# A hybrid encoder trunk on one core: the norm's affine part on VectorE, four raw weight buffers, and a newly searched order

## The chip, the core and the metric

The kernel runs on one core of one Trainium2 chip. The core has five engines that work side by side, each through its own queue in order: TensorE (PE) for matmuls, with its weight loads shown as PEld; VectorE (DVE); ScalarE (ACT); GpSimd (POOL); and SyncE (SP), which here only issues DMA transfers from the chip's memory (HBM) into the core's on-chip memory. Engines wait for each other through semaphores. The metric is the time of one execution in microseconds (us). Times of a kernel are given as the median of several runs; the profile is of one execution more, which has a time and a span (first to last instruction) of its own.

## The reference

Two layers act on x of 256 tokens by 1024 channels, in float32. Each layer:

```
z = x @ w_in[l]                                   # 1024 x 7440, split into the parts below
y_a = differential attention(aq, ak, av)          # 4 heads, all 256 keys
y_b = gated delta net(q, k, v, gate, a, b)        # convolution, then a triangular solve and a scan, both directions
y_c = windowed attention(cq, ck, cv)              # 8 heads, +-128 tokens
proj = einsum('btnc,ncd->btnd', stack(y_a, y_b, y_c), w_branch)
h = sum(sigmoid(gz) * proj) @ w_out
x = layer_norm(ALPHA * x + h, ln1_g, ln1_b)       # the first norm
gate, up = split(x @ w_up); gate = conv3(gate) + conv_b
f = (silu(gate) * up) @ w_down                    # the FFN, 2816 wide
x = layer_norm(ALPHA * x + f, ln2_g, ln2_b)       # the second norm
```

`layer_norm(v, g, b)` is `(v - mean) * rsqrt(var + 1e-5) * g + b` over the 1024 channels.

## The kernel before, in words

**Weights.** All large weights are packed on the host into blocks of 128 x 1024 float32 (512 KB). Each block is streamed once, in a fixed order, by SP. The function `weights` (and `take`, which calls it) brings a block in: a DMA into one of the `raw` buffers, of which there are RBUFS; ACT (or DVE, whichever the planner takes) rounds it to a shorter format as `hi`; DVE subtracts, `lo = raw - hi`, a pass of 128x1024. There are four buffers each of `hi` and `lo`. A raw buffer is free for the next load when `lo` is made. The activations are split alike: x in channel-major form is `xTh` and `xTl`. Each product is three matmuls, `hi*hi`, `hi*lo` and `lo*hi`, into the same PSUM bank (`mm3`). `proj_ch` makes channel-major products of a block pair; `token_major` makes token-major ones; `proj_tok` makes the two products that end in a norm (`wo` after the mixers, `fd` after the FFN), in 512-wide halves and for the two token tiles tt = 0, 1. The last blocks are kept, so that tt = 0 is done first, and the norm of tt = 0 runs beside the matmuls of tt = 1.

**The norm.** `Norm.part` adds the product to `ALPHA * x` and takes statistics on DVE. `Norm.tail` aggregates them, takes the power -0.5 of the variance on GpSimd (`pow_nhalf`, tile `s_tail`), makes the normalized `xh` (`q_tail` in the profile) on DVE, transposes it on PE (`ch_tail`, `at_tail`), applies gain and bias per channel (`e_tail`), and splits the result into `xTh` and `xTl`; the next matmuls need these. `Norm.finish` makes the same normalized values in token-major form: x = xh * gain + bias, in place, for the residual sum of the next norm, one whole half-layer later. Gain and bias stand spread over all partitions in four `ya` buffers of 128 x 512, loaded by `ln_params` with DMAs that GpSimd issues. `finish` runs for three of the four norms (the last writes its output itself): two tiles, two halves, two passes, eight instructions of 128x512 a norm, 24 in all.

**The order.** Nothing is issued when the code is read. Every call is recorded in `Plan` as an operation with an engine (or two to choose from, `either`), a price from `_cost`, and what it depends on. `Plan.emit` gives each operation a rank: the length of the longest chain of prices and latencies from it to the end, plus `urgent` (HASTE 60 or HASTE0 39 in the tails, BOOST 8 for weights), plus an entry of the table PRIO that belongs to its label, such as `(1, 'solve')` or `(0, 'gz', 8)`. `Plan.schedule` then simulates the five engines: it always takes the operation that can start first by the simulation, and among those that can start at the same moment on an engine the one of highest rank. The order that comes out is the order of each engine's queue on the chip; within a queue nothing overtakes. Weight blocks keep their stream order (`ORDER`), and PRIO moves a block's other work. A DMA is simulated as an issue, a transfer (`_cost`), a latency (`op.lat`) and, where a buffer has to come free first, DMA_ISSUE more. The simulation slows PE to half for a slot of 3.41 us (TICK) after a slot with little matmul work.

Every operation is issued from one helper, so all lines of the profile say L191; the tiles tell the instructions apart (`lo_take` is the `lo` of a block, `s_tail` the small tiles of a tail, and so on). GpSimd also makes the decay matrices of the delta net (`x_decay`, `D_decay`, `N_decay`) and small powers.

Of the kernel before, what the change touches and what calls it, by code (L numbers as in the profile page):

```python
# [10 lines left out]
F32 = mybir.dt.float32  # L11
F32R = mybir.dt.float32r
# [3 lines left out]
ALU = mybir.AluOpType  # L16
# [3 lines left out]
P = 128  # L20
# [25 lines left out]
SPOT = {('ft', 0, 0): 'g', ('ft', 0, 1): 'g', ('ft', 0, 2): 'yc', ('ft', 1, 0): 'g', ('ft', 1, 1): 'g', ('ft', 1, 2): 'yc', ('av', 1, 0): 'h16'}  # L46
DIRECT = False
WHOLE = ()
PRIO = {(1, 'a', 0): 2.3, (0, 'ckv', 0): -3.3, (0, 'gz', 8): 4.3, (1, 'wb', 7): -1.6, (0, 'k', 'ab', 0): 1.4, (1, 'cq', 0): 2.7, (0, 'gz', 9): -1.8, (1, 'k', 'q', 1): 8.1, (0, 'gz', 7): -2.0, (1, 'solve'): -4.6, (1, 'c', 'cq', 0): 2.5, (1, 'k', 'k', 1): -2.8, (0, 'aq', 1): -5.9, (0, 'gz', 3): 3.5, (0, 'ab', 0): -7.3, (0, 'gz', 10): 1.9, (0, 'c', 'ckv', 0): 1.8, (0, 'c', 0): -2.1, (0, 'k', 'gate', 1): 0.2, (0, 'q', 0): -7.1, (0, 'a', 2): 3.4, (1, 'v', 0): -4.1, (1, 'gz', 7): -1.0, (1, 'a', 'aq', 0): 4.5, (0, 'k', 0): -6.2, (0, 'q', 1): -7.6, (0, 'solve'): -2.7, (1, 'aq', 1): -4.7, (1, 'a', 'aq', 1): -1.4, (0, 'wb', 1): -0.6, (1, 'q', 1): 5.3, (0, 'gate', 0): 7.8, (0, 'a', 0): -0.7, (0, 'wb', 7): -1.0, (1, 'k', 'v', 0): -6.5, (1, 'wb', 2): 3.6, (0, 'a', 3): 2.0, (1, 'c', 0): 3.5, (1, 'k', 'v', 1): -5.3, (0, 'k', 'v', 1): -8.6, (1, 'c', 3): 3.4, (1, 'gate', 1): 5.4, (1, 'scan'): -1.6, (1, 'a', 2): 6.9, (1, 'av', 0): 5.6, (1, 'wb', 9): 2.5, (1, 'gz', 6): 1.6, (0, 'gz', 0): 1.3}
LOADS = (11, 12, 12)  # L50
PIECES = 2
PAIRS = ("s", "yc")
# [7 lines left out]
           "ACT": {"PE": 0.27, "ACT": 0.14, "DVE": 0.14, "POOL": 0.18, "SP": 1.42},  # L60
           "DVE": {"PE": 0.26, "ACT": 0.2, "DVE": 0.13, "POOL": 0.18, "SP": 1.22},
           "POOL": {"PE": 0.2, "ACT": 0.15, "DVE": 0.1, "POOL": 0.11, "SP": 0.2}}
DMA_ISSUE = 1.2
TICK = 10.24 / 3
FULL = 3060
ENGINES = ("PE", "ACT", "DVE", "POOL", "SP")
# [5 lines left out]
def _columns(ap):  # L72
    return math.prod(c for _, c in ap.ap[1:])


def _cost(eng, name, outs, ins, args, kw):

    n = max(_columns(ap) for ap in (outs[:1] + ins))
    if name == "dma_start":
        return 1.04 if eng == "POOL" else max(0.1, math.prod(c for _, c in outs[0].ap) * 4 / 3.6e5)  # L80
    if eng == "PE":
        if outs[0].offset // outs[0].ap[0][0]:
            return 0.0223
        wide = outs[0].dtype == F32 and ins[0].dtype == F32
        n = _columns(outs[0])
        slow = 4 if wide and name != "transpose" or ins[0].dtype == F32R and n < 256 else 2 if wide else 1
        return max(n * slow / 2400, 0.025) + 0.0023
    psum = [ap.space == PSUM for ap in outs[:1] + ins]
    if eng == "ACT":
        t = (0.05 if any(psum) else 0.093) + _columns(outs[0]) / 1200  # L90
        return t + 0.093 * sum(isinstance(kw.get(k), bass.AP) for k in ("scale", "bias", "accum_out"))
    if name == "memset":
        return 0.035 + n / 1200 if eng == "POOL" else 0.01 + n * SIZES[outs[0].dtype] / 3840
    if eng == "POOL":
        if kw.get("op") == ALU.pow:
            return 0.3 + 0.165 * n
        return (0.06 + n / 960) if name == "affine_select" else 0.1 + n / 570
    full = [ap for ap in ins if _columns(ap) > 1]
    fast = 1
    if len(full) == 1 and not any(psum) and name in ("tensor_copy", "tensor_scalar"):  # L100
        fast = 4 if full[0].dtype == F16 else 2
    return 0.069 + n / 960 / fast + 0.061 * sum(_columns(ap) == 1 for ap in ins)
# [26 lines left out]


class _Op:
    __slots__ = ("eng", "call", "cost", "deps", "known", "outs", "lat", "tiles", "new", "rank", "table", "start", "end", "urgent", "ways", "succ", "left", "ready", "group", "banks", "load", "columns", "label")


class Plan:
# [43 lines left out]
    def record(self, *ways):  # L179
        op = _Op()  # L180
# [10 lines left out]
            op.ways.append((eng, lambda fn=fn, args=args, kw=kw: fn(*args, **kw), _cost(eng, name, outs, ins, args, kw), table))  # L191
# [94 lines left out]
    def schedule(self, users, order):  # L286
# [38 lines left out]
        while done < len(ops):  # L325
# [25 lines left out]
            s, e, i = best  # L351
# [130 lines left out]
def tile_encoder_trunk(ctx: ExitStack, tc: tile.TileContext, a: dict, out: bass.AP, depth=DEPTH, tap=None):  # L482
# [252 lines left out]
    class Norm:  # L735
# [755 lines left out]
```

## Time and profile before

| | us |
|---|---|
| median of 3 runs (1015.25 to 1017.8) | 1015.89 |
| the profiled execution, time | 1016.1 |
| its span | 1014.4 |
| PE busy | 977.3 |
| DVE busy | 744.0 |
| ACT busy | 578.1 |
| GpSimd busy | 113.6 |

The stages in time: layer 0's mixers up to about 290 us, its first norm at 304 to 330, its FFN to 500, its second norm at 500 to 530; layer 1's mixers to about 780, the norm at 800 to 840, the FFN to 1005, and the last norm with the output to 1014.

How to read the rows: a row of a timeline has its start, its duration, the engine, the operation, the tiles as out<-in, shape and count, and in brackets the engine's idle time before it and who ended that. Rows of groups have `x` count, busy us, mean ns, and then idle time before them. Rows of tiles have the shortest, median and longest duration in ns. A row of stages has, for each engine, busy us and, in brackets, instructions; then the granted share of PE's clock. A busy PE overlaps its matmuls, so its busy time is not time at its peak.

### The profile page before, as it was taken

The numbers are of one execution on the slowest core, as the hardware profiler recorded it, in microseconds if no ns is written. First come the engines' busy times: TensorE is split into PE (matmuls) and PEld (weight loads), VectorE is DVE, ScalarE is ACT, GpSimd is POOL, SyncE is SP. The second block draws the span as 40 slices with busy tenths as digits, with TensorE's granted clock in tenths as the row PEclk, the third lists the DMA queues.
The fourth block names the chain that finished last, engine by engine and source line by source line (L and its number), as shares of the span: only waits on it lengthen the run. The fifth ranks groups of instructions, "written<-read, shape, count | busy, mean of one in ns | idle before, by whom it ended". The sixth has DMA issues, their size and how long they took to land. (4 is left out here: it accounts for less than half of the span.)

```text
span 1014.4 us, 19166 instructions
## 1 busy us (share of the span) xinstructions
PE 977.3 (96%) x7598; PEld 909.8 (90%) x7598; DVE 744.0 (73%) x1324; ACT 578.1 (57%) x1026; POOL 113.6 (11%) x108
## 2 busy tenths in 40 slices
PE   7998999999998999999989999999999989999996
PEld 5897899998986999998869989999999779999885
DVE  6789886775589777665679998875657878667555
ACT  5665864785355565553535776766644536555432
POOL 0510002100005100000144200001000150000000
PEclk9999999999999999999999999999999999999998
DMA  7552434464573765665625444334546746555661
GB/s 233 188 169 82 127 100 146 162 202 121 184 219 114 225 205 185 184 186 185 211 84 162 146 133 141 93 112 128 178 136 198 231 145 201 181 188 184 192 192 67
DMA packets 50109, 165.43 MB, mean 163 GB/s; under 512 B 5751, under 2 KB 11271, under 8 KB 50020
## 3 DMA queue, kind: packets, MB, share of 16 engines
q1 hardware_dynamic: 48644, 159.78, 49.7%
q0 software_dynamic: 1376, 4.43, 1.6%
q8 instruction: 59, 0.97, 0.4%
q14 instruction: 30, 0.25, 0.1%
HBM read 163.12 MB, written 1.07 MB: 162 GB/s over the span
## 5 line engine op out<-in xcount | busy, mean ns | idle before, releaser
L191 PE MATMUL mm_proj_ch<-xTh,lo_take 128*128 128x256 f32 x1488 | 420.1, 285 | 2.2 <-DVE lo_take L191 2.2
L191 PE MATMUL mm_proj_ch<-xTh,hi_take 128*128 128x256 f32 x1488 | 420.1, 285 | 0.9 <-ACT hi_take L191 0.9
L191 PE MATMUL mm_proj_ch<-xTl,hi_take 128*128 128x256 f32 x1488 | 418.1, 284 | 2.0 <-DVE xTl L191 2.0
L191 DVE TENSOR_TENSOR lo_take<-raw_take,hi_take 128x1024 fp32r<-128x1024 f32 x219 | 271.3, 1244 | 117.2 <-ACT hi_take L191 106.4
L191 ACT ACTIVATE hi_take<-raw_take 128x1024 fp32r<-128x1024 f32 x213 | 225.5, 1059 | 226.4 <-PE mm_proj_ch L191 143.4
L191 PEld LDWEIGHTS mm_proj_ch<-xTh,lo_take 128*128 128x128 f32 x1488 | 279.7, 189 | 5.5 <-DVE lo_take L191 4.1
L191 PEld LDWEIGHTS mm_proj_ch<-xTl,hi_take 128*128 128x128 f32 x1488 | 279.2, 189 | 5.7 <-DVE xTl L191 3.4
L191 PEld LDWEIGHTS mm_proj_ch<-xTh,hi_take 128*128 128x128 f32 x1488 | 279.7, 189 | 2.6 <-ACT hi_take L191 1.6
L191 DVE TENSOR_TENSOR lo_proj_tok<-raw_proj_tok,hi_proj_tok 128x1024 fp32r<-128x1024 f32 x50 | 61.2, 1225 | 49.2 <-ACT hi_proj_tok L191 49.0
L191 ACT ACTIVATE hi_proj_tok<-raw_proj_tok 128x1024 fp32r<-128x1024 f32 x50 | 53.1, 1061 | 74.1 <-PE mm_run L191 33.8
L191 POOL TENSOR_TENSOR s_tail<-s_tail,nhalf 128x1 f32<-128x1 f32 x8 | 6.8, 855 | 367.8 <-DVE s_tail L191 367.8
L191 DVE SCALAR_TENSOR_TENSOR z_conv_silu<-mm_proj_ch,col_params,z_conv_silu 128x254 f32<-128x254 f32 (+1 forms) x96 | 39.6, 473 | 0.5 <-ACT z_conv_silu L191 0.4
L191 ACT ACTIVATE e_window<-e_window,s_window 128x256 f32<-128x256 f32 x57 | 27.2, 498 | 7.3 <-DVE s_window L191 7.2
L191 POOL DMA_DIRECT2D ya_ln_params<-in_lnp_dram x16 | 8.8, 554 | 188.3 <-PE mm_product L191 96.6
L191 DVE SCALAR_TENSOR_TENSOR g_product<-g_product,mm_product 128x512 f32<-128x512 f32 x24 | 16.3, 683 | 16.3 <-PE mm_product L191 16.2
L191 PE MATMUL mm_run<-hi_proj_tok,ile_encoder_trunk 128*128 128x512 f32 x88 | 27.3, 389 | 0.0
L191 PE MATMUL mm_run<-hi_proj_tok,tile_encoder_trunk 128*128 128x512 f32 x88 | 27.3, 389 | 0.0
L191 ACT ACTIVATE e_attention<-e_attention,s_attention 128x256 f32<-128x256 f32 x48 | 23.3, 500 | 5.6 <-DVE s_attention L191 5.6
L191 PEld LDWEIGHTS <-h_solve 128*128 128x128 f16 x448 | 20.7, 99 | 5.6 <-issue 2.8
L191 PE MATMUL mm_product<-yc_window,hi_take 128*128 128x256 f32 x128 | 24.0, 284 | 1.1 <-DVE yc_window L191 0.6
L191 PE MATMUL mm_product<-ya_attention,hi_take 128*128 128x256 f32 x128 | 24.4, 286 | 0.0
L191 POOL TENSOR_TENSOR x<-q_tail,ya_ln_params 128x512 f32<-128x512 f32 x12 | 22.2, 1865 | 11.2 <-DVE q_tail L191 11.2
(344 smaller groups left out, 1714.9 us busy)
## 6 DMA issues: line engine op xcount, KB each, us to landing
raw_take<-in_w_dram SPq DMA_DIRECT2D x226, 512.0 KB, 3.7
raw_proj_tok<-in_w_dram SPq DMA_DIRECT2D x60, 512.0 KB, 3.6
G_load_G<-band SPq DMA_DIRECT2D x24, 192.0 KB, 3.5
ya_ln_params<-in_lnp_dram POOLq DMA_DIRECT2D x16, 256.0 KB, 6.2
x<-in_xT_dram SPq DMA_DIRECT2D x4, 256.0 KB, 4.2
x<-in_x_dram SPq DMA_DIRECT2D x2, 512.0 KB, 4.5
out_dram<-x SPq DMA_DIRECT2D x8, 128.0 KB, 1.8
_tile_encoder_trunk<-in_w_dram SPq DMA_DIRECT2D x4, 128.0 KB, 3.7
```

What stands on the lines that cost most here:

```text
L191: op.ways.append((eng, lambda fn=fn, args=args, kw=kw: fn(*args, **kw), _cost(eng, name, outs, ins, args, kw), table))
```

## The change

Four edits. `Norm.finish` issues its 24 passes on VectorE in place of GpSimd. `RBUFS` goes from 3 to 4. PRIO is replaced by another table with 100 entries in place of 48. And the planner's prices, which the order comes from, are changed: of DMAs (issue, transfer, latency), of float32 and fp32r matmuls, of GpSimd's powers; and where a DVE operation and a GpSimd operation would run at the same time in the simulation, the one that starts later is made longer. The arithmetic of the kernel is the same.

```diff
-RBUFS = 3
+RBUFS = 4
...
-PRIO = {(1, 'a', 0): 2.3, (0, 'ckv', 0): -3.3, (0, 'gz', 8): 4.3, (1, 'wb', 7): -1.6,
...
+PRIO = {(0, 'a', 'ak', 0): 2.8, (0, 'a', 'aq', 0): 1.5, (0, 'a', 'aq', 1): -8.3, (0, 'a', 1): 9.2,
...
-DMA_ISSUE = 1.2
+DMA_ISSUE = 0.3
...
     if name == "dma_start":
-        return 1.04 if eng == "POOL" else max(0.1, math.prod(c for _, c in outs[0].ap) * 4 / 3.6e5)
+        return 0.55 if eng == "POOL" else max(0.45, math.prod(c for _, c in outs[0].ap) * 4 / 3.9e5)
     if eng == "PE":
         if outs[0].offset // outs[0].ap[0][0]:
             return 0.0223
-        wide = outs[0].dtype == F32 and ins[0].dtype == F32
-        n = _columns(outs[0])
-        slow = 4 if wide and name != "transpose" or ins[0].dtype == F32R and n < 256 else 2 if wide else 1
-        return max(n * slow / 2400, 0.025) + 0.0023
+        n, w = _columns(outs[0]), _columns(ins[0])
+        if ins[0].dtype == F32R and n >= 256:
+            return max(n * 17 / 16 / 2400, 0.119 if w == P else 0.113)
+        if ins[0].dtype in (F32, F32R):
+            passes = 1 if name == "transpose" else 2
+            return passes * max(n * 2 / 2400 + 0.0023, 0.112) * (1.35 if w < P and n > P else 1)
+        return max(n / 2400, 0.025) + 0.0023
...
     if eng == "POOL":
         if kw.get("op") == ALU.pow:
-            return 0.3 + 0.165 * n
+            return 0.65 + 0.13 * n
         return (0.06 + n / 960) if name == "affine_select" else 0.1 + n / 570
...
-        op.lat = (3.0 if eng == "POOL" else 0.91) if name == "dma_start" else None
+        op.lat = (3.5 if eng == "POOL" else 2.6) if name == "dma_start" else None
...
+        beside = {"DVE": 0.0, "POOL": 0.0}
...
+            if e == "DVE" and op.sbuf:
+                cost += min(cost, max(0.0, beside["POOL"] - s))
+                beside[e] = s + cost
+            elif e == "POOL" and not op.lat:
+                cost += 0.6 * min(cost, max(0.0, beside["DVE"] - s))
+                beside[e] = s + cost
...
                     for c in range(2):
                         xs = x[:, tt, c * 512:(c + 1) * 512]
-                        G.tensor_tensor(xs, self.xh[tt][c], self.gb[c], op=ALU.mult)
-                        G.tensor_tensor(xs, xs, self.gb[2 + c], op=ALU.add)
+                        V.tensor_tensor(xs, self.xh[tt][c], self.gb[c], op=ALU.mult)
+                        V.tensor_tensor(xs, xs, self.gb[2 + c], op=ALU.add)
```

`op.sbuf` is true for operations whose operands all stand in the on-chip memory SBUF and that are at least 64 columns wide.

More of the change, by code (lines that the diff above doesn't have):

```diff
@@ L48 @@
 WHOLE = ()
-PRIO = {(1, 'a', 0): 2.3, (0, 'ckv', 0): -3.3, (0, 'gz', 8): 4.3, (1, 'wb', 7): -1.6, (0, 'k', 'ab', 0): 1.4, (1, 'cq', 0): 2.7, (0, 'gz', 9): -1.8, (1, 'k', 'q', 1): 8.1, (0, 'gz', 7): -2.0, (1, 'solve'): -4.6, (1, 'c', 'cq', 0): 2.5, (1, 'k', 'k', 1): -2.8, (0, 'aq', 1): -5.9, (0, 'gz', 3): 3.5, (0, 'ab', 0): -7.3, (0, 'gz', 10): 1.9, (0, 'c', 'ckv', 0): 1.8, (0, 'c', 0): -2.1, (0, 'k', 'gate', 1): 0.2, (0, 'q', 0): -7.1, (0, 'a', 2): 3.4, (1, 'v', 0): -4.1, (1, 'gz', 7): -1.0, (1, 'a', 'aq', 0): 4.5, (0, 'k', 0): -6.2, (0, 'q', 1): -7.6, (0, 'solve'): -2.7, (1, 'aq', 1): -4.7, (1, 'a', 'aq', 1): -1.4, (0, 'wb', 1): -0.6, (1, 'q', 1): 5.3, (0, 'gate', 0): 7.8, (0, 'a', 0): -0.7, (0, 'wb', 7): -1.0, (1, 'k', 'v', 0): -6.5, (1, 'wb', 2): 3.6, (0, 'a', 3): 2.0, (1, 'c', 0): 3.5, (1, 'k', 'v', 1): -5.3, (0, 'k', 'v', 1): -8.6, (1, 'c', 3): 3.4, (1, 'gate', 1): 5.4, (1, 'scan'): -1.6, (1, 'a', 2): 6.9, (1, 'av', 0): 5.6, (1, 'wb', 9): 2.5, (1, 'gz', 6): 1.6, (0, 'gz', 0): 1.3}
+PRIO = {(0, 'a', 'ak', 0): 2.8, (0, 'a', 'aq', 0): 1.5, (0, 'a', 'aq', 1): -8.3, (0, 'a', 1): 9.2, (0, 'a', 2): 3.9, (0, 'a', 3): 0.9, (0, 'ab', 0): -2.6, (0, 'ak', 0): 3.5, (0, 'ak', 1): 4.0, (0, 'aq', 1): 2.2, (0, 'c', 'ckv', 0): 2.5, (0, 'c', 0): -0.4, (0, 'c', 3): 0.1, (0, 'ckv', 0): 1.0, (0, 'cq', 0): 2.7, (0, 'cq', 1): -5.7, (0, 'finish'): 1.9, (0, 'gate', 0): 2.4, (0, 'gate', 1): -3.8, (0, 'gz', 0): 3.5, (0, 'gz', 1): 12.2, (0, 'gz', 10): 4.7, (0, 'gz', 3): 2.4, (0, 'gz', 4): -3.8, (0, 'gz', 5): 0.5, (0, 'gz', 6): -0.8, (0, 'gz', 7): 2.6, (0, 'gz', 8): 5.4, (0, 'gz', 9): -0.7, (0, 'k', 'gate', 1): -0.4, (0, 'k', 'k', 0): -0.2, (0, 'k', 'k', 1): -2.6, (0, 'k', 'q', 1): 6.5, (0, 'k', 0): 4.6, (0, 'k', 1): 0.3, (0, 'q', 1): 3.8, (0, 'scan'): -2.2, (0, 'solve'): 1.6, (0, 'v', 1): 10.8, (0, 'wb', 0): 3.5, (0, 'wb', 1): -2.3, (0, 'wb', 10): 2.3, (0, 'wb', 11): 1.1, (0, 'wb', 2): -0.9, (0, 'wb', 4): 3.3, (0, 'wb', 6): -1.2, (0, 'wb', 7): 4.8, (0, 'wb', 9): -4.7, (1, 'a', 'ak', 0): -3.6, (1, 'a', 'ak', 1): 1.8, (1, 'a', 'aq', 0): -0.6, (1, 'a', 'aq', 1): 2.6, (1, 'a', 0): 6.1, (1, 'a', 1): 9.7, (1, 'a', 2): -0.1, (1, 'a', 3): 5.0, (1, 'ak', 1): 1.3, (1, 'aq', 1): -5.2, (1, 'av', 0): -4.0, (1, 'c', 'ckv', 0): 5.6, (1, 'c', 'cq', 0): -0.9, (1, 'c', 0): 3.4, (1, 'c', 1): 4.6, (1, 'cq', 0): 0.3, (1, 'cq', 1): 4.0, (1, 'finish'): -8.5, (1, 'gz', 0): 0.4, (1, 'gz', 1): 0.5, (1, 'gz', 10): 8.7, (1, 'gz', 11): -3.8, (1, 'gz', 2): -25.8, (1, 'gz', 3): -4.1, (1, 'gz', 5): 2.9, (1, 'gz', 6): 3.0, (1, 'gz', 7): -0.5, (1, 'gz', 9): 1.5, (1, 'k', 'ab', 0): -9.2, (1, 'k', 'gate', 0): 1.1, (1, 'k', 'gate', 1): 6.2, (1, 'k', 'k', 0): -1.5, (1, 'k', 'k', 1): -2.3, (1, 'k', 'q', 0): -9.5, (1, 'k', 'q', 1): -1.8, (1, 'k', 'v', 0): 2.2, (1, 'k', 'v', 1): -4.1, (1, 'k', 0): 0.7, (1, 'k', 1): -4.5, (1, 'q', 0): -1.2, (1, 'q', 1): -7.8, (1, 'scan'): -8.2, (1, 'solve'): -1.2, (1, 'v', 0): 2.7, (1, 'wb', 0): 2.0, (1, 'wb', 11): -0.6, (1, 'wb', 2): 1.6, (1, 'wb', 3): -8.2, (1, 'wb', 5): 0.6, (1, 'wb', 6): 6.2, (1, 'wb', 7): 10.1, (1, 'wb', 8): 9.3}
@@ L131 @@
 class _Op:
-    __slots__ = ("eng", "call", "cost", "deps", "known", "outs", "lat", "tiles", "new", "rank", "table", "start", "end", "urgent", "ways", "succ", "left", "ready", "group", "banks", "load", "columns", "label")
+    __slots__ = ("eng", "call", "cost", "deps", "known", "outs", "lat", "tiles", "new", "rank", "table", "start", "end", "urgent", "ways", "succ", "left", "ready", "group", "banks", "load", "columns", "label", "sbuf")
 class Plan:
@@ L220, in record @@
         op.urgent, op.label = self.urgent, self.label
+        op.sbuf = all(ap.space == bass.MemoryType.SB for ap in outs[:1] + ins) and _columns(outs[0]) >= 64
         self.ops.append(op)
```

## The prediction, made before the changed kernel ran

> **What bounds the kernel now.** I read the page first, then busy times by stage, then the timeline of the three norms, then the waits.
>
> ```profile
> span 1014.4 us, 19166 instructions
> PE 977.3 (96%) x7598; PEld 909.8 (90%) x7598; DVE 744.0 (73%) x1324; ACT 578.1 (57%) x1026; POOL 113.6 (11%) x108
> PE 32%; issue 7%; DVE 4%; DMA 1%; ACT 1%; POOL 1%; POOLq 0%; DVEq 0%; ACTq 0%; SPq 0%
> core 0: us, PE busy (x) PEld busy (x) DVE busy (x) ACT busy (x) POOL busy (x), PEclk, DMA share, GB/s
> 75.00:130.00 55.00, 50.52 (x590) 46.92 (x589) 49.04 (x104) 37.21 (x72) 1.32 (x3) 0.97 0.34 106
> 304.00:330.00 26.00, 22.43 (x99) 16.92 (x97) 24.90 (x45) 13.22 (x27) 13.64 (x10) 0.93 0.36 116
> 330.00:460.00 130.00, 130.00 (x1033) 127.28 (x1034) 89.72 (x123) 72.60 (x93) 2.73 (x5) 1.00 0.64 198
> 500.00:530.00 30.00, 26.77 (x135) 20.44 (x134) 24.78 (x42) 12.96 (x25) 15.48 (x10) 0.94 0.29 93
> 530.00:575.00 45.00, 44.14 (x355) 42.81 (x354) 41.94 (x71) 29.50 (x56) 17.71 (x16) 1.00 0.56 176
> 575.00:640.00 65.00, 62.28 (x704) 59.01 (x703) 60.31 (x137) 47.50 (x93) 2.66 (x4) 1.00 0.38 117
> 800.00:840.00 40.00, 36.70 (x205) 30.47 (x204) 31.20 (x58) 18.07 (x33) 17.21 (x14) 0.96 0.50 159
> 840.00:945.00 105.00, 105.00 (x877) 104.47 (x877) 74.36 (x99) 60.53 (x79) 0.00 (x0) 1.00 0.60 190
> ```
>
> PE is busy for 977.3 of 1014.4 us, so the whole gain without less matmul work lies in the other 37.1 us and in the few slots where the granted clock (column PEclk) falls below 1. In the two long FFN stretches (330 to 460, 840 to 945) PE is busy all the time, and what DVE does there (89.72 of 130 us and 74.36 of 105) is free. The losses stand elsewhere. The ends of the three norms with a successor (304 to 330, 500 to 530, 800 to 840) leave PE idle for 3.57, 3.23 and 3.30 us and run at a granted 0.93, 0.94 and 0.96. The stretches around the delta-net solve (75 to 130, 575 to 640) leave 4.48 and 2.72 us, and there DVE is busy for 49.04 of 55 and 60.31 of 65 us: it is the second bound.
>
> The timeline of DVE, and then of PE, around the norms shows why PE stands there.
>
> ```profile
> 313.21 1.52 DVE L191 TENSOR_TENSOR xTl<-e_tail,xTh 128x256 fp32r<-128x256 f32 x1
> 314.66 3.46 DVE L191 TENSOR_TENSOR yc_weights<-raw_take,yc_weights 128x512 fp32r<-128x512 f32 x2
> 509.54 2.81 DVE L191 TENSOR_TENSOR xTl<-e_tail,xTh 128x256 fp32r<-128x256 f32 x2
> 512.27 0.68 DVE L191 SCALAR_TENSOR_TENSOR x<-x,ch_run 128x512 f32<-128x512 f32 x1
> 514.13 0.41 DVE L191 TENSOR_TENSOR xTl<-e_tail,xTh 128x256 fp32r<-128x256 f32 x1
> ```
>
> ```profile
> 318.50 0.78 PE L191 MATMUL mm_token_major<-g_weights,xTl 128*128 128x512 f32 x1 [2.04 <-DVE xTl L191]
> 326.67 0.51 PE L191 MATMUL mm_proj_ch<-xTl,hi_take 128*128 128x256 f32 x2 [1.51 <-DVE xTl L191]
> 506.66 1.87 PE L191 MATMUL ch_run<-g_weights,tile_encoder_trunk 128*128 128x512 f32 x7
> 510.98 0.50 PE L191 MATMUL mm_token_major<-hi_take,xTl 128*128 128x512 f32 x1 [0.58 <-DVE xTl L191]
> 515.46 0.44 PE L191 MATMUL ch_tail<-tri,q_tail 128*128 128x128 f32 x2 [2.10 <-DVE q_tail L191]
> 818.98 0.44 PE L191 MATMUL ch_tail<-tri,q_tail 128*128 128x128 f32 x2 [2.13 <-DVE q_tail L191]
> ```
>
> The same 128x256 `xTl` subtraction takes 0.41 us at 514.13, and 1.52 at 313.21; two of them at 509.54 take 2.81, and two `yc_weights` of 128x512, 3.46. The long ones stand beside these GpSimd instructions:
>
> ```profile
> L191 POOL TENSOR_TENSOR x<-q_tail,ya_ln_params 128x512 f32<-128x512 f32 x12 | 22.2, 1865 | 11.2 <-DVE q_tail L191 11.2
> L191 POOL TENSOR_TENSOR x<-x,ya_ln_params 128x512 f32<-128x512 f32 x12 | 16.9, 1430 | 0.0
> 815.25 2.71 POOL L191 TENSOR_TENSOR x<-x,ya_ln_params 128x512 f32<-128x512 f32 x2
> 817.92 0.55 POOL L191 TENSOR_TENSOR s_tail<-s_tail,nhalf 128x1 f32<-128x1 f32 x1
> 825.12 2.20 POOL L191 DMA_DIRECT2D ya_ln_params<-in_lnp_dram  x4
> 815.86 0.15 DVE L191 TENSOR_SCALAR s_tail<-s_tail 128x1 f32<-128x1 f32 x1
> ```
>
> These 24 instructions, 39.1 us, are the norm's affine part. At the first norm they stretch `xTl` by 1.1 us and the `yc_weights` pair to 3.46, and PE waits 2.04 us for the `xTl` behind them. At the second the last `ch_run` matmul is done at 508.53, but DVE takes its sum up only at 512.27, behind `xTl` passes with 2.0 us too much; PE then waits 2.10. At the third the variance is ready at 816.01 (815.86 + 0.15), and the power that follows starts at 817.92, behind two affine passes in GpSimd's own queue; PE waits 2.13.
>
> **Part 1: the affine part on DVE.** Removed: 24 GpSimd instructions. Added: 24 DVE instructions of the same shape. The trace has such sums on DVE:
>
> ```profile
> L191 DVE TENSOR_TENSOR g_product<-g_product,g_product x16: 681/691/693, 247.5 to 789.9; 128x512 f32<-128x512 f32 x16
> 517.00:518.00 1.00, 1.00 (x5) 0.70 (x4) 1.00 (x3) 0.00 (x0) 1.00 (x2) 0.50 0.00 0
> ```
>
> The first row gives 0.691 us at the median, so 16.6 us in all, 5.5 at each norm. What may come back is at most the whole idle time of the three windows, 3.57 + 3.23 + 3.30 = 10.1 us, and the time lost to the granted clock, 0.07 x 26 + 0.06 x 30 + 0.04 x 40 = 5.2 us (in the second row the clock stands at 0.50 just after the wait of 2.10). At least it is nothing: then the tail's own chain of statistics, power, transposes and split is as long without the collisions. Of the waits named above, which end in the DVE work that the collisions delay, 2.04 + 1.51 (at 326.67) + 0.58 + 2.10 + 2.13 = 8.4 us. The chain of the tail remains behind them, so I take three quarters of these, 6.3, and half of the clock, 2.6: 8.9 us. By the Trainium skill, TensorE: Matmul & The Clock Gate, section "What's actually happening", the half rate follows a whole idle window of about 3.4 us; here it follows a wait of 2.10, so the trace disagrees. By the page no clock would come back with such short waits, and the sum would be 2.6 us worse.
>
> Against it stands the DVE time. At the first and third norms the eight moved instructions can run in the FFN stretch, beside a PE that is busy anyway; without that cover they cost up to 11 us. At the second, layer 1 starts: DVE is busy for 41.94 of 45 us and then 60.31 of 65. Of 5.5 us I charge half, 2.8, since DVE is also rid of that norm's stretched passes (2.0 us in the row at 509.54 alone). Net gain of part 1: 8.9 - 2.8 = 6.1 us; from -16.6 (nothing hidden, nothing regained) to +15.3.
>
> In GpSimd's queue the power comes free of the passes. The next norm's parameter loads (825.12) stand behind them as before: their buffers are those that the passes read, so they now wait for DVE's last pass, and in the FFN nothing urgent is queued behind them on GpSimd, which is busy for 2.73 us in 330 to 460. What is late next, once these waits go: the weight splits of the first projection after each norm, which stand behind the tail on DVE.
>
> **Part 2: the fourth raw buffer.** A weight block lands in a raw buffer, ACT makes `hi`, DVE makes `lo`, and only then may SP start the next load into it. Nothing is added but loads that start earlier, in the one SP queue, so the next load's wait moves ahead of the bias-table loads queued behind it.
>
> ```profile
> SPq L191 <- DVE lo_take L191: 569.3, 190, 16.9
> ACT hi_take L191 <- DMA raw_take<-in_w_dram: 38.0, 21, 10.0
> L191 PE MATMUL mm_proj_ch<-xTh,lo_take 128*128 128x256 f32 x1488 | 420.1, 285 | 2.2 <-DVE lo_take L191 2.2
> 827.73 6.67 DMA raw_take<-in_w_dram
> raw_take<-in_w_dram SPq DMA_DIRECT2D x226, 512.0 KB, 3.7
> ```
>
> SP waits 190 times for `lo_take` to free a buffer, and ACT 38.0 us for landings; but PE's matmuls on `lo`, the later of the two halves, waited for it 2.2 us in all, because four split buffers lie between. So the gain is between 0 and these 2.2 us. The loss is bounded by one late landing a norm: 6.67 - 3.7 = 3.0 us at 827.73, if more loads in flight slow each other, so 9.0. I take +1.0, nearer to PE's rows than to ACT's.
>
> **Part 3: the order.** The planner (a list scheduler) gets new prices and a new table of priorities, so nearly every queue is reordered. No row shows an order that has not run. The upper bound is the idle time of the dense stretches, 4.48 + 0.86 + 2.72 = 8.1 us, and 0.03 x 55 = 1.7 us of clock: 9.7. Below, I take the same size as a loss, since the same DVE work in a worse order can leave PE idle twice as long. The prices decide the sign for me. A weight load was priced at 1.46 + 0.91 = 2.4 us from issue to use, and is now 1.34 + 2.6 = 3.9, where the row says 3.7. The power of one column was 0.47 and is 0.78; the eight in the trace took 0.86 on average:
>
> ```profile
> L191 POOL TENSOR_TENSOR s_tail<-s_tail,nhalf 128x1 f32<-128x1 f32 x8 | 6.8, 855 | 367.8 <-DVE s_tail L191 367.8
> ```
>
> An affine pass on GpSimd was priced at 0.1 + 512/570 = 1.0 where the rows say 1.87 and 1.43, and DVE's passes beside it at no loss. An order made with prices nearer to the rows should leave instructions less often in a queue behind one that isn't ready. I take +4.0, somewhat under half of the bound.
>
> **The sum.** The profiled execution took 1016.1 us (1014.4 and 1.7 around it), 0.2 more than the median of 1015.89. 1016.1 - 6.1 - 1.0 - 4.0 = 1005.0, or 1004.8 against the median. Forecast: 1005 us, 1.1% less.
>
> **The rivals.**
>
> *The order brings nothing, the buffer neither.* Then only part 1 counts: 1015.9 - 6.1 = 1010. For it: PE's own waits for weights are small, and the solve stretches are bound by DVE's work, which no order makes less. Against: the waits of 4.48 and 2.72 us do not fill those stretches. This holds too if the fourth buffer changes nothing.
>
> *The collisions move instead of going.* GpSimd keeps the decay work, right after the second norm, and the moved passes read the same memory from DVE:
>
> ```profile
> L191 POOL TENSOR_TENSOR x_decay<-tri,gh_gdn_scalars 128x512 fp32r<-128x512 f32 x4 | 6.2, 1570 | 21.1 <-PE ch_gdn_scalars L191 20.4 <-PE ch_decay L191 0.7
> L191 DVE TENSOR_TENSOR lo_take<-raw_take,hi_take 128x1024 fp32r<-128x1024 f32 x15 | 20.9, 1390 | 1.4 <-ACT hi_take L191 1.4
> L191 DVE TENSOR_TENSOR lo_take<-raw_take,hi_take 128x1024 fp32r<-128x1024 f32 x10 | 12.2, 1220 | 1.8 <-ACT hi_take L191 1.7
> ```
>
> The first two rows are of 530 to 575, the third of 75 to 130: `lo_take` takes 1.39 us beside the decay and 1.22 away from it. If four of the eight moved passes each meet an `x_decay` and wait 1.57, DVE gets 5.5 + 6.3 us in a stretch that has 3.06 free; the 8.7 us above that stand on PE's path. Part 1 is then 8.9 - 8.7, and with an order that brings nothing the buffer is all that is left: 1015. The Trainium skill, SBUF — State Buffer, section "Who interferes with whom", speaks for this rival: a DVE instruction with two SBUF inputs contends with a GpSimd one that reads SBUF, and the second blocks until the first is done. The stretched rows agree. Against: each moved pass leaves GpSimd, where it met DVE's passes at this same price.
>
> *All comes back.* The boundaries return 15.3 - 2.8 = 12.5, the order 8, the buffer 1: 994. For it: the waits named above all end on DVE. Against: part of it is the tail's own chain.
>
> *Slower: the weight splits starve.* The place is the DVE-bound stretches of both layers, with 10 + 15 `lo_take` in the two of 75 to 130 and 530 to 575 alone. An order that puts one more 0.69 us pass ahead of a split makes PE wait that long, once the split buffers have run empty. It decides from 7.1 / 0.69 = 10 such splits on, when it has eaten parts 1 and 2; at 20 of these 25, 13.8 us: 1015.9 - 7.1 + 13.8 = 1022.6. For it: DVE has only 3.06 + 4.69 us free in 110, and 5.5 us of new work arrives. Against: the planner prices just this.
>
> **How the numbers follow.** About 0.3%, 3 us, is what a measurement of this kernel can tell from no change. Forecast 0.38 (1000 to 1009 as its own range), part 1 alone 0.18, collisions moved 0.13, all back 0.12, slower 0.19. Faster by more than 3 us: 0.38 + 0.18 + 0.12 + 0.01 from the edge of the collisions, 0.69; no change 0.12; slower 0.19. The range goes up to 1020, with half of the slower case left out (0.10), and down to 991, below which lies about half of "all back" (0.06); with 0.84 it holds a little more than asked, because no row bounds a new order.
>
> **What would show it.** Right: no GpSimd `x` pass at the norms, `xTl` back at 0.41 to 0.42 us everywhere there, a power that starts 0.03 us after its variance, PE idle under 2 us a norm window, and granted clock near 1. For part 2: ACT's wait for landings well under 38 us. For part 3: less PE idle time in 75 to 130 and 575 to 640. Wrong: the 24 passes between tail instructions on DVE, `xTl` beside `x_decay` at 1.4 us, or longer PE waits for `lo_take` in layer 1.

## The result, and the profile after

The changed kernel takes 1000.29 us (median of 5 runs, 999.95 to 1000.59); the kernel before, 1015.96 (median of 5 runs, 1015.25 to 1017.84). The ratio is 0.984, with a 95% interval from 0.9826 to 0.9855. That is 4.7 us less than the 1005 predicted and inside the likeliest case's own range, 1000 to 1009. The profiled execution took 1000.26 us with a span of 998.6, so the span is 15.8 us shorter.

First the page of the changed kernel, then its stages in the columns of the prediction's (busy us of each engine with its instructions, then the granted clock):

```profile
span 998.6 us, 19140 instructions
PE 972.1 (97%) x7598; PEld 909.3 (91%) x7598; DVE 741.0 (74%) x1362; ACT 568.5 (57%) x1012; POOL 72.4 (7%) x84
```

```profile
75.00:130.00 55.00, 51.25 (x619) 48.14 (x618) 52.64 (x116) 38.53 (x72) 1.32 (x3) 1.00 0.37 116
304.00:330.00 26.00, 25.57 (x168) 22.04 (x167) 24.79 (x53) 14.66 (x26) 0.67 (x1) 1.00 0.47 152
500.00:530.00 30.00, 29.30 (x198) 25.69 (x197) 26.86 (x63) 16.95 (x27) 5.67 (x3) 1.00 0.37 120
530.00:575.00 45.00, 43.97 (x402) 42.47 (x401) 41.20 (x82) 30.52 (x67) 13.88 (x15) 1.00 0.46 149
575.00:640.00 65.00, 61.51 (x675) 58.34 (x673) 58.05 (x124) 42.94 (x99) 4.03 (x5) 1.00 0.36 113
800.00:840.00 40.00, 39.80 (x280) 36.48 (x279) 31.77 (x58) 21.99 (x34) 2.86 (x5) 1.00 0.57 183
```

DVE is busy for 741.0 us where it was busy for 744.0: 24 passes came in addition and the total did not rise, which fits with other passes that are no longer stretched.

The three norm windows leave PE idle for 0.43 + 0.70 + 0.20 = 1.3 us, where they left 10.1: 8.8 us less. The granted clock is 1.00 in all three; before it lost 5.2 us there, and 0.03 x 55 = 1.7 us in 75 to 130, where it is 1.00 now too. Together that is 15.7 us, the size of the whole difference. Items of both signs cancel beside it: the first 40 us of the kernel have 2.0 us more of PE's work in them, and 640 to 780 is 0.9 us emptier. The stretches around the solve give nothing: idle 3.75 + 1.03 + 3.49 = 8.3 us, where it was 4.48 + 0.86 + 2.72 = 8.1 (less in 75 to 130, more behind it).

Windows at fixed times hold different work in the two kernels. An estimate that goes by work instead (each matmul of the two traces counted with the distance to the next that is usual for its form in the trace before) has the changed kernel 4.8 us ahead at 304 us; it wins 4.8, 5.3 and 5.4 us more in the three norm windows, and falls back by 4.2 us between 530 and 780. So the items that cancel are not small: about what is won ahead of the first norm is lost again in layer 1's mixers.

The groups of DVE: the tile's splits in the kernel before, the same in the changed kernel, and one half of the moved passes (count, busy us, mean ns, idle time before):

```profile
L191 DVE TENSOR_TENSOR xTl<-e_tail,xTh 128x256 fp32r<-128x256 f32 x24 | 16.9, 735 | 0.0
L194 DVE TENSOR_TENSOR xTl<-e_tail,xTh 128x256 fp32r<-128x256 f32 x24 | 9.3, 421 | 0.4 <-ACT xTh L194 0.4
L194 DVE TENSOR_TENSOR x<-q_tail,ya_ln_params 128x512 f32<-128x512 f32 x12 | 7.8, 692 | 0.0
```

The 24 `xTl` passes take 0.42 us on average, where they took 0.735; the stretched one at 313.21 took 1.52. The moved passes take 0.692 us, the 0.691 of the row that priced them. The timelines of DVE and GpSimd at the third norm show where they run:

```profile
803.85 0.16 DVE L194 TENSOR_SCALAR s_tail<-s_tail 128x1 f32<-128x1 f32 x1
804.09 0.67 POOL L194 TENSOR_TENSOR s_tail<-s_tail,nhalf 128x1 f32<-128x1 f32 x1 [7.95 <-DVE s_tail L194]
812.12 1.89 DVE L194 TENSOR_TENSOR x<-q_tail,ya_ln_params 128x512 f32<-128x512 f32 x3
813.93 1.22 DVE L194 TENSOR_TENSOR lo_take<-raw_take,hi_take 128x1024 fp32r<-128x1024 f32 x1
815.07 1.89 DVE L194 TENSOR_TENSOR x<-x,ya_ln_params 128x512 f32<-128x512 f32 x3
```

The variance is ready at 804.01 (803.85 + 0.16) and the power starts 0.08 us later; before it stood 1.91 us in GpSimd's queue (816.01 to 817.92). Six of the eight passes run between weight splits after the tail (812.12, 815.07), where PE has blocks in hand. The next norm's parameter loads start at 813.71 on GpSimd, behind DVE's passes, which read their buffers; PE is idle for 0.20 us in all in that window. The row of `hi_take`'s landings in the waits of the changed kernel (total us, times, longest):

```profile
ACT hi_take L194 <- DMA raw_take<-in_w_dram: 7.8, 9, 1.9
```

ACT's wait for these landings fell from 38.0 to 7.8 us.

### The profile page after: what moved, and what is told of

The parts are those of the page before. It is cut to its first block, busy times and chain, and to the rows that moved or that the text cites. A ratio compares the mean times of both kernels' runs of the same rounds, so it can differ in the third digit from the quotient of the medians.

```text
span 998.6 us, 19140 instructions
## 1 busy us (share of the span) xinstructions
PE 972.1 (97%) x7598; PEld 909.3 (91%) x7598; DVE 741.0 (74%) x1362; ACT 568.5 (57%) x1012; POOL 72.4 (7%) x84
## 4 chain that ended last, share of the span: by engine, by line
PE 79%; DVE 9%; ACT 6%; DMA 3%; issue 2%; POOL 1%; POOLq 0%; ACTq 0%; DVEq 0%
PE mm_proj_ch L194 47%; PE mm_run L194 7%; PE ch_run L194 7%; PE mm_product L194 5%; PE mm_token_major L194 4%; PE at_window L194 2%; DVE lo_take L194 2%; DVE h_solve L194 2%; ACT hi_take L194 1%; DMA G_load_G<-band 1%; PE at_attention L194 1%; DVE z_conv_silu L194 1%; DMA raw_take<-in_w_dram 1%; PE ch_gdn L194 1%; PE ch_solve L194 1%
## 5 line engine op out<-in xcount | busy, mean ns | idle before, releaser
L194 ACT ACTIVATE hi_take<-raw_take 128x1024 fp32r<-128x1024 f32 x213 | 223.2, 1057 | 236.4 <-PE mm_proj_ch L194 172.5
L194 DVE TENSOR_TENSOR lo_take<-raw_take,hi_take 128x1024 fp32r<-128x1024 f32 x219 | 267.5, 1232 | 87.7 <-ACT hi_take L194 83.7
L194 PE MATMUL mm_product<-ya_gdn,hi_take 128*128 128x256 f32 x128 | 23.4, 282 | 0.0
L194 PE MATMUL ch_run<-hi_proj_tok,ile_encoder_trunk 128*128 128x512 f32 x72 | 22.5, 389 | 0.0
```

## The experiments

Twelve kernels were timed, in three groups, each group on one chip beside the kernel before (medians there 1016.97, 1017.24 and 1017.04 us). Differences in us below are between medians of one group. Where a kernel is compared with the changed one, or with one of another group, the ratios to the kernel before are subtracted and taken of 1016 us. "Replanned" means that the planner made a new order for the edited code. Some edits keep an order instead: the planner sees the old operation and the chip gets the new one.

### Part 1 alone, in a new order and in the old one

The affine part goes to DVE in the kernel before, replanned with its own prices and table:

```diff
-                        G.tensor_tensor(xs, self.xh[tt][c], self.gb[c], op=ALU.mult)
-                        G.tensor_tensor(xs, xs, self.gb[2 + c], op=ALU.add)
+                        V.tensor_tensor(xs, self.xh[tt][c], self.gb[c], op=ALU.mult)
+                        V.tensor_tensor(xs, xs, self.gb[2 + c], op=ALU.add)
```

> The kernel before with one edit: the 24 affine passes on DVE, planned anew with the old prices and the old priorities, three raw buffers. Theory (the collisions of the affine passes with the norm's tail cost the time): the three norm windows lose most of their 10.1 us of idle time and 5.2 us of clock, less up to 5.5 us in the DVE-bound start of layer 1: 1003 to 1009, with xTl at 0.42 us all through. Rival (the new order and its prices brought the gain): 1013 to 1018.

And the same with every operation at the place in the order that it had before:

```diff
-                        G.tensor_tensor(xs, self.xh[tt][c], self.gb[c], op=ALU.mult)
...
+                        plan.record(("POOL", "tensor_tensor", nc.vector.tensor_tensor, (xs, self.xh[tt][c], self.gb[c]), {"op": ALU.mult}))
...
```

> The kernel before with its order kept on PE, ACT and SP; only the 24 passes are issued on DVE, at their place in the old order (which knew them as GpSimd's). Theory: the collisions and the power's wait go, but the passes stand in DVE's queue where they come, so some tail instructions wait 0.69 us each: 1004 to 1011. Rival (only a new order helps): 1014 to 1020, since the passes now delay the tail directly.

Measured: replanned 1008.53 us (ratio 0.9915, 0.9884 to 0.9945), 8.4 us less; in the old order 1009.02 (0.9928, 0.9902 to 0.9954), 8.0 less. The stages of the two, the one in the old order first:

```profile
304.00:330.00 26.00, 23.83 (x114) 17.80 (x113) 24.80 (x56) 14.19 (x28) 1.61 (x2) 1.00 0.39 125
500.00:530.00 30.00, 28.18 (x156) 22.07 (x155) 23.55 (x57) 15.59 (x30) 1.69 (x2) 1.00 0.38 117
800.00:840.00 40.00, 37.61 (x236) 32.10 (x235) 34.12 (x70) 20.67 (x34) 3.89 (x6) 1.00 0.56 184
```

```profile
304.00:330.00 26.00, 25.59 (x143) 21.25 (x142) 24.09 (x52) 13.92 (x29) 1.61 (x2) 1.00 0.51 165
500.00:530.00 30.00, 29.47 (x184) 25.11 (x183) 28.59 (x64) 18.44 (x36) 5.54 (x7) 1.00 0.37 119
530.00:575.00 45.00, 40.82 (x328) 40.40 (x328) 34.11 (x60) 23.61 (x47) 13.98 (x11) 0.96 0.48 153
800.00:840.00 40.00, 39.12 (x246) 33.96 (x245) 35.66 (x69) 23.85 (x41) 3.81 (x6) 1.00 0.61 199
```

In the old order the norms' idle time falls from 10.1 to 2.17 + 1.82 + 2.39 = 6.4 us, and the clock of this execution is 1.00 in all three windows, where 5.2 us were lost: 8.9 together, the very sum that was predicted. Not all of it is time won. PE's order is the same in both kernels, so their traces can be followed matmul by matmul: part 1 wins 2.2, 2.6 and 2.1 us at the three norms, about 7 in all, and 0.3 us are lost between 530 and 780. This execution (1011.28 us, the slowest of its four) is 1.4 us behind from its start, where its clock is low once, at 21.5 us; so it is only 4.8 us faster than the traced one of before.

Replanned, the idle time falls further, to 0.41 + 0.53 + 0.88 = 1.8, so 13.5 us come back with the clock by the same count of windows. But the traced execution (1010.08, again the slowest of four) is only 6.0 us faster than that of before. The main place of the loss is the start of layer 1: 530 to 575 has 4.18 us of idle time where it had 0.86, and a clock of 0.96, about 5 us together. First GpSimd's queue there in the replanned kernel, then DVE's in the same time, then PE's wait:

```profile
527.98 1.04 POOL L191 TENSOR_TENSOR x_decay<-tri,gh_gdn_scalars 128x512 fp32r<-128x512 f32 x1
529.84 6.40 POOL L191 TENSOR_TENSOR x_decay<-tri,gh_gdn_scalars 128x512 fp32r<-128x512 f32 x1 [0.81 <-PE ch_decay L191]
```

```profile
529.44 1.28 DVE L191 TENSOR_TENSOR x_decay<-tri,gl_gdn_scalars 128x512 fp32r<-128x512 f32 x2
...
531.84 3.48 DVE L191 TENSOR_TENSOR lo_take<-raw_take,hi_take 128x1024 fp32r<-128x1024 f32 x3
```

```profile
PE ch_decay L191 <- POOL x_decay L191: 4.2, 1, 4.2
```

One `x_decay` pass takes 6.40 us, the pass of the same shape just ahead of it 1.04. It ends at 536.24, 0.92 us after a row of DVE passes that follow each other without a gap (529.44 to 535.32: two `x_decay`, a `z_conv_silu`, another `x_decay`, three `lo_take`), none of them stretched. PE's decay matmul waits 4.2 us for it. This is the rival "the collisions move", with one difference: it is not DVE's passes that pay at this place, but the GpSimd pass. The changed kernel has the four `x_decay` passes in one row. They meet DVE's passes too (8.65 us for the four, 3.31 for the longest), but PE waits only 0.3 us for them. Its timeline of GpSimd:

```profile
524.92 8.65 POOL L194 TENSOR_TENSOR x_decay<-tri,gh_gdn_scalars 128x512 fp32r<-128x512 f32 x4 [23.10 <-DVE gh_gdn_scalars L194]
```

### Part 1 taken back

In the changed kernel the two lines go back to GpSimd, replanned:

```diff
-                        V.tensor_tensor(xs, self.xh[tt][c], self.gb[c], op=ALU.mult)
-                        V.tensor_tensor(xs, xs, self.gb[2 + c], op=ALU.add)
+                        G.tensor_tensor(xs, self.xh[tt][c], self.gb[c], op=ALU.mult)
+                        G.tensor_tensor(xs, xs, self.gb[2 + c], op=ALU.add)
```

> The changed kernel with the 24 passes back on GpSimd, planned anew with the new prices and priorities, four raw buffers. Theory: the tails collide again, 1008 to 1013. Rival (the order brought the gain, and a planner that prices collisions plans around them): 1000 to 1004.

And in the changed kernel's own order on PE, ACT and SP, with only the 24 passes issued on GpSimd:

```diff
-                        V.tensor_tensor(xs, self.xh[tt][c], self.gb[c], op=ALU.mult)
...
+                        plan.record(("DVE", "tensor_tensor", nc.gpsimd.tensor_tensor, (xs, self.xh[tt][c], self.gb[c]), {"op": ALU.mult}))
...
```

> The changed kernel's order kept to the instruction on PE, ACT and SP; only the 24 passes are issued on GpSimd at their place in the order in place of DVE. Nothing but the engine of the passes differs. Theory: DVE's passes at the norms are stretched to 1.4 us again, the power waits behind passes, PE idles 3 us a norm window and the clock drops: 1008 to 1014. Rival: 1000 to 1003.

Measured: replanned 1014.39 us (0.9983, 0.9969 to 0.9997); in the changed kernel's order 1023.0 (1.0056, 1.0037 to 1.0075). Against the changed kernel's 0.984 that is 14.5 and 21.9 us more, and both are above their expected ranges. The stages of the second, then DVE's, PE's and GpSimd's timelines at its first norm:

```profile
304.00:330.00 26.00, 20.75 (x105) 16.45 (x104) 22.42 (x36) 9.01 (x19) 11.61 (x9) 0.87 0.29 101
500.00:530.00 30.00, 26.43 (x144) 20.90 (x144) 21.34 (x44) 13.62 (x28) 13.78 (x9) 0.94 0.28 89
800.00:840.00 40.00, 35.25 (x189) 29.39 (x188) 34.48 (x59) 19.06 (x35) 17.76 (x14) 0.91 0.55 179
```

```profile
312.21 3.16 POOL L194 TENSOR_TENSOR x<-q_tail,ya_ln_params 128x512 f32<-128x512 f32 x2
312.86 2.98 DVE L194 TENSOR_SCALAR q_tail<-x,s_tail,s_tail 128x256 f32<-128x256 f32 x3
320.32 0.39 PE L194 MATMUL mm_proj_ch<-xTl,hi_take 128*128 128x256 f32 x1 [1.58 <-DVE xTl L194]
322.75 2.15 DVE L194 TENSOR_TENSOR xTl<-e_tail,xTh 128x256 fp32r<-128x256 f32 x3
324.28 0.58 PE L194 MATMUL mm_proj_ch<-xTl,hi_take 128*128 128x256 f32 x1 [1.88 <-DVE xTl L194]
```

Three `q_tail` passes take 2.98 us beside two GpSimd passes; the changed kernel's same three took 1.05, by its timeline of DVE:

```profile
313.64 1.05 DVE L194 TENSOR_SCALAR q_tail<-x,s_tail,s_tail 128x256 f32<-128x256 f32 x3
```

Three `xTl` passes take 2.15 beside four GpSimd passes (5.28 us from 318.67), and PE waits 1.58 and 1.88 for `xTl`. The norms' idle time is 5.25 + 3.57 + 4.75 = 13.6 us, and the clock falls to 0.87, 0.94 and 0.91. Followed matmul by matmul, the two executions with the same order on PE part by 6.8, 5.5 and 7.5 us at the three norms and run nearly side by side everywhere else (0.7 us at most). So the mechanism of part 1 is shown in both directions: the passes on GpSimd stretch the tail, and the tail is PE's path.

### The fourth raw buffer

Alone in the kernel before, replanned:

```diff
-RBUFS = 3
+RBUFS = 4
```

> The kernel before with a fourth raw buffer alone, planned anew with the old prices. Theory (the split buffers already cover late landings): 1014 to 1017. Rival (the buffer is worth several us by itself): under 1012.

Taken from the changed kernel, replanned:

```diff
-RBUFS = 4
+RBUFS = 3
```

> The changed kernel with three raw buffers, planned anew with the new prices and priorities. Theory: the buffer is worth 0 to 2 us of the 15.7, so 1000 to 1002.5. Rival (the new order rests on loads that run further ahead): 1004 to 1010.

Measured: 1024.24 us (1.0061, 1.0042 to 1.008), 7.0 *more* than before; and 1019.31 (1.0019, 1.0005 to 1.0033), 18.2 more than the changed kernel. Neither is in the range of its theory or of its rival. Both cannot be the price of a buffer: each edit also makes the planner write a new order. So the buffer was given to the chip alone, in orders planned for three, once in that of the last kernel (there RBUFS is set to 3 for the planner as well) and once in that of the kernel before:

```diff
-        t = pool.tile(list(shape), dtype, tag=tag, name=name, bufs=bufs)
+        t = pool.tile(list(shape), dtype, tag=tag, name=name, bufs=bufs + (tag == "raw"))
```

> The order of the run with three raw buffers and all else as changed (1019.3), kept to the instruction on every engine, but with four raw buffers behind it: loads may run one block further ahead, nothing else. Theory (the 19 us of that run lie in the order that the planner makes for three buffers): 1014 to 1019. Rival (they lie in loads that come late): 1001 to 1010.

> The kernel before with its order kept on every engine and four raw buffers behind it. Theory (the loads are hidden; planning anew for four buffers with the old prices cost the 7 us of the run with the buffer alone): 1013 to 1017. Rival 1 (more loads in flight slow each other): 1020 or more. Rival 2 (the buffer is worth several us by itself): under 1012.

Measured: 1012.07 us (0.9946, 0.9927 to 0.9965) against a ratio of 1.0019 with three buffers in the same order: 7.4 us less. These two ran on different chips, and their intervals allow 4 to 11 us. In the order before: 1010.48 (0.9941, 0.9924 to 0.9958), 6.6 less. The buffer itself is worth about 7 us, and within these intervals the two orders agree on it; both are faster than the ranges of their theories. Where it comes from shows, for the order before, ahead of the first norm. The timelines of ACT, DVE and PE, first of the kernel before:

```profile
16.02 1.06 ACT L191 ACTIVATE hi_take<-raw_take 128x1024 fp32r<-128x1024 f32 x1 [2.54 <-DMA raw_take<-in_w_dram]
17.12 0.74 PE L191 MATMUL mm_token_major<-hi_take,xTh 128*128 128x512 f32 x2 [0.90 <-ACT hi_take L191]
30.65 0.17 DVE L191 CAST gh_gdn_scalars<-gg_gdn_scalars 128x16 fp32r<-128x16 f32 x1
34.52 0.50 PE L191 MATMUL ch_decay<-x_decay,strict 128*128 128x512 f32 x1 [0.32 <-DVE x_decay L191]
35.97 0.50 PE L191 MATMUL ch_decay<-x_decay,strict 128*128 128x512 f32 x1 [0.60 <-DVE x_decay L191]
37.83 0.39 PE L191 MATMUL mm_token_major<-hi_take,xTl 128*128 128x512 f32 x1
294.04 1.06 ACT L191 ACTIVATE hi_proj_tok<-raw_proj_tok 128x1024 fp32r<-128x1024 f32 x1 [2.12 <-DMA raw_proj_tok<-in_w_dram]
295.67 0.50 PE L191 MATMUL mm_run<-hi_proj_tok,kk_product 128*128 128x512 f32 x1 [0.69 <-ACT kk_product L191]
309.59 0.38 PE L191 MATMUL ch_tail<-tri,q_tail 128*128 128x128 f32 x2
```

and the same instructions with the fourth buffer in the same order:

```profile
14.15 1.06 ACT L191 ACTIVATE hi_take<-raw_take 128x1024 fp32r<-128x1024 f32 x1 [1.03 <-DMA raw_take<-in_w_dram]
28.10 0.17 DVE L191 CAST gh_gdn_scalars<-gg_gdn_scalars 128x16 fp32r<-128x16 f32 x1
34.44 0.39 PE L191 MATMUL mm_token_major<-hi_take,xTl 128*128 128x512 f32 x1
304.28 0.38 PE L191 MATMUL ch_tail<-tri,q_tail 128*128 128x128 f32 x2
313.18 0.50 PE L191 MATMUL mm_token_major<-g_weights,xTl 128*128 128x512 f32 x1 [2.29 <-DVE xTl L191]
```

ACT's `hi_take` waits 2.54 us for a landing in the first and 1.03 in the second. PE pays for it at once: it waits 0.90 us for this `hi_take` at 17.12 and not at all with the fourth buffer, which is 1.5 us ahead by 19 us. Everything behind the late ones in ACT's queue is late too, and DVE's small chain behind that: `gh_gdn_scalars`, which the decay needs, comes at 30.65 against 28.10. PE then waits 0.32 and 0.60 us, and those waits are booked to `x_decay`, a tile that has nothing to do with weights. By the `mm_token_major` matmul at 37.83 against 34.44 the buffer is 3.4 us ahead. Matmul by matmul, the lead then stays flat until about 285 us and grows again in the `wo` product: before, ACT waits 2.12 us for a landing at 294.04, and PE 0.69 for the `kk_product` that stands behind it in ACT's queue. At the first transpose of the norm, 309.59 against 304.28, the lead is 5.3. The waits of `hi_take` for landings add up to 6.0 us in this kernel, 38.0 before; PE's waits for `lo_take` are what they were, 2.1 us against 2.2.

In the other order the place is not shown. Its two traced executions differ by only 3.2 us (1016.81, the fastest of ten with three buffers, against 1013.59), and at 45 us the one with four buffers is 0.75 us behind.

### Prices and table

The changed kernel with the old table, and with an empty one:

```diff
-PRIO = {(0, 'a', 'ak', 0): 2.8, (0, 'a', 'aq', 0): 1.5, (0, 'a', 'aq', 1): -8.3, (0, 'a', 1): 9.2,
+PRIO = {(1, 'a', 0): 2.3, (0, 'ckv', 0): -3.3, (0, 'gz', 8): 4.3, (1, 'wb', 7): -1.6,
...
```

> The changed kernel with the old table of priorities; passes on DVE, four raw buffers, new prices. Theory of the prediction (prices nearer to the rows give the better order): 1001 to 1004, the priorities worth 1 to 4 us. Rival (the searched priorities carry the second half of the gain): 1006 to 1011, about where the passes on DVE with the old prices stand (1008.5).

```diff
-PRIO = {(0, 'a', 'ak', 0): 2.8, (0, 'a', 'aq', 0): 1.5, (0, 'a', 'aq', 1): -8.3, (0, 'a', 1): 9.2,
...
+PRIO = {}
```

> The changed kernel with an empty table of priorities: new prices, passes on DVE, four raw buffers. Theory (prices nearer to the rows make the better order): 1003 to 1010, clearly under the next run. Rival (the searched table does it): 1010 to 1020, no better than the next run.

The changed kernel with the old prices and the new table (the DMA, PE and power prices of before, and no price of a collision):

```diff
-DMA_ISSUE = 0.3
+DMA_ISSUE = 1.2
...
-            if e == "DVE" and op.sbuf:
-                cost += min(cost, max(0.0, beside["POOL"] - s))
-                beside[e] = s + cost
...
```

> The changed kernel with the old prices; passes on DVE, four raw buffers, new priorities. Theory of the prediction (the prices decide): the new priorities mean little without them, 1006 to 1011. Rival (priorities decide): 1000 to 1004.

The same with an empty table:

```diff
...
+PRIO = {}
...
```

> The same with the old prices: empty table, passes on DVE, four raw buffers. Theory: 1012 to 1024, at least 6 us over the run before it. Rival: within 3 us of it.

Measured:

| prices | table | us | ratio to before, 95% | over the changed kernel, us |
|---|---|---|---|---|
| new | new (the changed kernel) | 1000.29 | 0.9826 to 0.9855 | 0 |
| new | old | 1005.31 | 0.9857 to 0.99 | 3.9 |
| new | none | 1008.67 | 0.989 to 0.9941 | 7.7 |
| old | none | 1011.24 | 0.9924 to 0.9963 | 10.5 |
| old | new | 1021.34 | 1.0023 to 1.0051 | 20.0 |

The old table with the new prices lies between what the theory and the rival gave it. Without a table the two kernels of one group differ in the prices alone: 1011.24 - 1008.67 = 2.6 us, where the theory asked for at least 6. The difference is small, but the single times (1008.37 to 1009.46, and 1010.46 to 1013.25) do not overlap. One place where the two part is the layer-1 start, first with the old prices and no table, with its GpSimd pass, then with the new prices and no table:

```profile
530.00:575.00 45.00, 41.57 (x315) 40.32 (x313) 34.09 (x51) 26.10 (x50) 14.97 (x11) 0.92 0.48 154
```

```profile
530.40 6.31 POOL L191 TENSOR_TENSOR x_decay<-tri,gh_gdn_scalars 128x512 fp32r<-128x512 f32 x1 [1.08 <-PE ch_decay L191]
```

```profile
285.00:304.00 19.00, 15.75 (x64) 12.55 (x63) 14.93 (x23) 9.59 (x16) 2.19 (x4) 0.82 0.82 266
530.00:575.00 45.00, 44.46 (x361) 43.37 (x362) 41.06 (x70) 30.26 (x59) 19.72 (x16) 1.00 0.50 164
```

The old prices put one `x_decay` beside a row of DVE passes again (6.31 us), and the stretch has 3.4 us of idle time and a clock of 0.92; with the new prices it has 0.54 and 1.00. It is not the only one: the first 40 us have 7.36 us of idle time with the old prices and 5.59 with the new. Which of the prices brings the 2.6 us was not separated. Without a table both kernels lose time at 285 to 304, before the first norm: 3.25 us idle and a clock of 0.82 with the new prices, 3.99 and 0.82 with the old, where the changed kernel is close to full. The new table with the old prices is the worst of all, 10 us above the range that was expected; 285 to 304 has 3.89 us of idle time there too, and the largest hole is another:

```profile
575.00:640.00 65.00, 58.98 (x670) 54.96 (x669) 56.44 (x124) 45.78 (x97) 2.14 (x3) 0.95 0.30 96
```

A table is thus no list of important steps that holds by itself. It fits one program with one set of prices, and with any other it moves the time by up to 20 us.

## Why the prediction was right, and where its steps were off

*Bound and place.* Right. PE's idle time at the three norms and the clock behind it were the loss, and 14.0 of the 15.8 us come from there by the count of windows, 15.5 by the estimate that goes by work.

*Part 1, predicted 6.1 us.* Right in mechanism: with the order kept, the norms answer to the passes' engine in both directions. Measured 8.0 in the old order and 8.4 replanned; the intervals (4.7 to 10.0 and 5.6 to 11.8 us) hold the 6.1, so the size is not refuted. Its terms were off both ways. The waits were taken at 6.3 and gave 3.7 in the old order; the clock was taken at 2.6 and gave 5.2 in the traced execution. That the gross sum is 8.9 both times is luck. The charge of 2.8 us for DVE time at the layer-1 start was too high: with the order kept, 0.3 us were lost there and in all of layer 1's mixers. With a replanned order the loss at that place was about 5 us, but by a stretched GpSimd pass and not by want of DVE time.

*The power in GpSimd's queue.* Right: it starts 0.08 us after its variance (0.03 were predicted).

*Part 2, predicted 1.0 us with an upper bound of 2.2.* Wrong, by the step that took the bound from PE's own waits for `lo`. Measured 6.6 and 7.4 (interval in the old order, 4.3 to 7.7 by its ratio). The waits that set the bound did not even change (2.2, then 2.1). What went were waits behind late landings at the head of ACT's queue: one of 0.90 us for `hi`, and others that PE has under the names of tiles that come later in that queue or depend on it (`x_decay`, `kk_product`). The row with ACT's 38.0 us was in hand, and was given too little weight. The loss from loads that slow each other, 9.0 us at most, is not seen in the times.

*Part 3, predicted 4.0 us.* Its place was wrong: the idle time of the solve stretches, which gave the bound, did not fall (8.3 us after, 8.1 before). The 1.7 us of clock in 75 to 130 did come back, but they did so with part 1 in the old order as well (clock 1.00 there). For its reason, prices nearer to the rows, speak the 2.6 us without a table; which of the prices it was is not shown. Its size is not settled. Part 1 and the buffer, each alone in the old order, give 8.0 and 6.6; if they add, which was not run, the estimate is 1016 - 14.6 = 1001.4 us, and the new order would be worth about 1 us beside the old one, with several us of uncertainty by the two intervals. What the new order does is to give back at the norms what part 1 leaves there in the old order (6.4 us idle against 1.3); by the estimate that goes by work it loses 4.2 us between 530 and 780, where part 1 in the old order loses 0.3. How much of the 4.0 that makes stays open.

*The rivals.* "The order brings nothing, the buffer neither" is false in its second half. "The collisions move" came true with the old prices (`x_decay` 6.40 and 6.31 us), at the place named, and cost about 5 us in the first of these kernels; in the new order the longest is 3.31 us and PE hardly waits for it. "All comes back" (994) expected 8 us from the solve stretches, which gave none. "The splits starve" did not occur: PE's matmuls on `lo` wait 0.5 us in all. That the total was met at 0.5% is therefore partly luck: the buffer was sized too low by 5.6 us, part 1 perhaps by 2, and the order, if the parts add, too high by about 3.

## What to carry to other kernels

A wait is to be priced at the queue it holds up, and not only at the engine that matters: late landings at the head of ACT's in-order queue hid a gain of 6.6 us here, while PE's waits for `lo`, the row that set the bound, were 2.2 us and stayed. Two engines that read the same memory are to be priced together by whoever orders the work, and the engine that is not the bound can be the one that is stretched. And where an order is searched for, test an edit with the order kept as well as replanned: here a new plan alone moved the time by up to 20 us, three times what the buffer is worth.

## What was not expected of the hardware

A GpSimd pass of 1.04 us can last 6.40 us, and 6.31 and 5.91 us in two other kernels, while DVE runs passes without a gap. In all three it ends 0.90 to 0.92 us after the last `lo_take` of DVE's row, close to its own 1.04 us, as if it had run only when the row was done; that is inferred from the times. The Trainium skill, SBUF — State Buffer, section "Who interferes with whom", says that of a DVE instruction with two SBUF inputs and a GpSimd one that reads SBUF the second blocks until the first is done. Here the pass outlasted a whole row of DVE's, and the trace does not show why it did not come in between two of them.

The clock does not go by the length of the wait alone. In the trace before, it is low around the norms in three pieces of 3.4 us at 0.50, from 318.6, 516.5 and 820.3 us, each 0.1 to 1.3 us behind a PE wait of 2.04, 2.10 and 2.13. But the kernel with the fourth buffer in the same order waits 2.29 us at the matmul that had waited 2.04 (now at 313.18), and its window has 1.00:

```profile
304.00:330.00 26.00, 21.30 (x119) 16.73 (x119) 23.73 (x36) 10.83 (x22) 13.26 (x9) 1.00 0.34 106
```

It leaves PE idle for 4.70 us, more than the 3.57 before. So a clock of 1.00 in one traced execution is in part chance: part 1 in the old order has a piece at 21.5 us, in a stretch that the edit does not touch and where the trace before has none. It is not chance alone: the mean granted clock was 0.996 to 0.998 in the five runs of the changed kernel, and 0.989 to 0.996 in the runs of the kernel before beside the experiments. The Trainium skill, TensorE: Matmul & The Clock Gate, section "What's actually happening", has the gate look at whole windows of about 3.4 us. That would make the place of a wait within the window count, which agrees with this pair; waits as short as 2.0 us that do lose the clock do not agree with a window that must be idle throughout.
